# A hybrid decoder layer on one core: a recurrent block's end, the sample states, two recurrences and the last gates are put at other places

## The chip, the core and the metric

The kernel runs on one core of one Trainium2 chip. The core has a matrix engine (TensorE, PE in the profile; its weight loads are listed as PEld), a vector engine (VectorE, DVE), a scalar engine with function tables (ScalarE, ACT), a general one (GpSimd, POOL) and one that only issues transfers (SyncE, SP). Each runs its own instructions in order; semaphores tie them together. Matrix products accumulate in eight banks of PSUM, everything else works from SBUF; the large tensors lie in HBM and come and go by DMA. The metric is the device time of one launch in microseconds (us), less is better.

## What is computed

One layer with two groups of heads over 2048 prompt positions and 8 single-token samples, model width 1024. Cut to what matters here:

```python
hn = _rmsnorm(x, g_norm) * (1.0 + scale[:, None]) + shift[:, None]
z = hn @ w_in
xa, za, q, k, v, glr, zg = jnp.split(z, SPLITS, axis=-1)
# RG-LRU: 8 blocks of 128 channels
xc = conv_b + sum(xp[:, j:j + T] * conv_w[j] for j in range(CONV_W))
gx = jax.nn.sigmoid(xb @ w_gate_x + b_gate_x)          # per block
ga = jax.nn.sigmoid(xb @ w_gate_a + b_gate_a)
a = jnp.exp((LRU_C * ga) * jax.nn.log_sigmoid(lru_lambda))
u = jnp.sqrt(-jnp.expm1(2.0 * log_a)) * (gx * xc)
h = scan(a, u)                                          # h_t = a_t h_{t-1} + u_t
y_lru = h * jax.nn.silu(za)
# GLA: 4 heads, key width 128, value width 256
o, S_new = _gla_chunked(q, k, v, log_alpha, S0)         # S_t = diag(alpha_t) S_{t-1} + k_t^T v_t
o = o * lax.rsqrt(mean(o * o) + EPS) * g_gla_norm
y_gla = o * jax.nn.silu(zg)
x = x + gate * (concat(y_lru, y_gla) @ w_out)
```

The samples take the same layer with their own states: for each of the 8 samples and 4 heads a 128x256 state is read, updated and written.

## The kernel before

The prompt goes in two halves of 1024 positions. Each half walks over the four GLA heads, and puts RG-LRU blocks between them; a segment is 512 positions wide, or 384, 384 and 264 in the second half, where the 8 samples ride along at the end (in some blocks of the first half 512, 256 and 264). A projection (`project`, L661 to L663) is 24 matmuls into one accumulator bank: each operand is split into a high and a low part, and three of the four products are taken. Four PSUM banks rotate as `acc`, two as `tp`, and one each belongs to the head recurrence under the names `kv` and `o`.

An RG-LRU block projects its channels (`xa_unit`), convolves them on DVE (`conv`, L1278), splits the result into `xh` and `xl`, and multiplies these by two gate matrices (`gates`, L1315 to L1317); ACT takes the tanh of both (L1318). When the last segment's gates are in, `gates` goes on to the block's end: an exponential, a tanh and a square root on ACT (L1323, L1325, L1326, the last under another function table), three element-wise steps and the scan on DVE (L1330 to L1334). `out` (L1352) then multiplies the state by the gate value silu(za), which stands in one of four `zs` tiles, and `spill` (L675) sends the product to HBM from ACT's queue.

A head of the GLA group has its decays and its keys and queries (`gla_qk`), then the chunked recurrence: `gla_start` (transposes L1042 and L1045), one `gla_chunk` (L1068 to L1076) for each 128 positions, `gla_norm`, `gla_out` (transposes L1162). In the second half the samples' states follow: `sample_state` loads four states, ACT and DVE update them (L1104, L1105), `sample_out` multiplies them by the queries (L1114), writes them back, and after the second four takes the norm `os` that `gla_out` puts behind the last segment (L1164).

The order of the work on each engine is not that of the source alone. `after(n, f)` puts the function f into a list that falls due n units later, and `tick()`, called after each projection of up to 512 columns, advances the clock and calls what is due. A scheduler then orders each engine's instructions by estimated times; `behind(q)` holds an instruction's place after the last one that engine q has been given so far.

Between the halves some products are made in a cheaper way from sums of blocks of hn (`seven`): seven products instead of eight (named ZB11 to ZT4, matmuls L1559), whose operands are sums and differences of parts of hn that `sums` makes on DVE and ACT (L1491 to L1500, tiles `fs`, `ra`, `so`). The first such group is the gate values of a head (`gates_seven(0)`); the second is the channels of RG-LRU block 0 of the second half (`lru_seven(0)`), whose sums L1568 are written into the block's `xa` tile. `xa_new` makes the tiles of a block and puts the last three columns of the first half at the front of `xa` (L1385). There is one `xa` tile, so a new block writes where the one before it wrote. The last first-half RG-LRU block, number 7, ends shortly before, among the sums.

After the second half's heads, the last two RG-LRU blocks run together (`last_a`): their gates for all three segments are taken at once. `xp`, `lp`, `gp`, `sp_`, `st` are pools of SBUF tiles; the query weights of the first head stand in a tile `wq` of `st`, made at L471.

Of the kernel before, what the change touches and what calls it, by code (L numbers as in the profile page):

```python
# [8 lines left out]
F32 = mybir.dt.float32  # L9
# [5 lines left out]
P = 128  # L15
# [39 lines left out]
def hybrid_kernel(ctx, tc, i, o):  # L55
# [381 lines left out]
    with tc.tile_pool(name="ada", bufs=1, side="right") as ap:  # L437
# [31 lines left out]
        for t in range(2):  # L469
            SP.dma_start(xt45[t], i["x_prompt"][0, (4 + t) * P:(5 + t) * P])  # L470
        wkq0.append(weights(Q0 + HEADS[0] * DK, DK, both=st.tile([P, 2, D], F32R, name="wq"), later=True))  # L471
        x67 = x_pair(2)
# [240 lines left out]

    def flush_gla():
        while any(e[3] for e in pend):
            e = min(e for e in pend if e[3])
            pend.remove(e)
            heapq.heapify(pend)
            e[2]()

    def ada_gate():
# [369 lines left out]
    def sample_state(h, smp, b0, st, done):  # L1091
# [9 lines left out]
        for n in range(4):  # L1101
# [68 lines left out]
    def gla_head(half, h, wv=None, ahead=None):  # L1170
# [57 lines left out]
        for s in range(ns):  # L1228
            if wv and s == 0:
                prep[s] = prep0  # L1230
                pk = project(wk, 512, 512)
                rest()
            else:
                prep[s] = gla_qk(half, h, s, wq, wk, dec, pk)
                pk = None
                if s == 0 and ahead:
                    with held(V):
                        ahead()
            if s + 1 < ns:
# [22 lines left out]
    def lru_units(half, last_a=None, seven=False):  # L1262
# [42 lines left out]
        def gates(t, ss):  # L1305
            j, cv, xh, xl, wgh, wgl, res = t.j, t.cv, t.xh, t.xl, t.wgh, t.wgl, t.res
            if ss[0] == 0:
                t.tx, t.tg = t_("tx"), t_("tg")
            tx, tg = t.tx, t.tg
            for s in ss:  # L1310
                c0, sn = t.segs[s]
                c = slice(c0, c0 + sn)
                for g, (out, bias) in enumerate(((tx, hbx), (tg, hba))):
                    ps = acc()[:, :sn]
                    PE.matmul(ps, wgh[:, g], xh[:, c], start=True, stop=False)  # L1315
                    PE.matmul(ps, wgh[:, g], xl[:, c], start=False, stop=False)
                    PE.matmul(ps, wgl[:, g], xh[:, c], start=False, stop=True)  # L1317
                    S.activation(out[:, c], ps, AF.Tanh, bias=bias[:, j:j + 1], scale=0.5)  # L1318
# [88 lines left out]
        def za_unit(t, s):  # L1407
            c0, sn = t.segs[s]
            z = xp.tile([P, 512], F32, tag="f512", name="z5") if half == 1 and t.j == LRU_TILES[3][0] and s == 2 else None
            z = silu2(t.wz, c0, sn, z)  # L1410
            after(2, lambda: out(t, s, z))
            tick()

        if seven:
            return xa_load, xa_new, xa_unit, out
        return xa_load, xa_unit, za_load, za_unit
# [209 lines left out]
    def lru_seven(j):  # L1626
        xa_load, xa_new, xa_unit, out = lru_units(1, seven=True)
        t = xa_load(j, [None])
# [9 lines left out]

        seven(len(HEADS) - 1 + j, use, lambda s: t.xa[:, 3 + s * 512:3 + s * 512 + 512])

# [618 lines left out]
```

## Time and profile before

| | |
|---|---|
| median of 3 runs | 1452.09 us (1451.66 to 1459.42) |
| the profiled execution, its whole time | 1452.05 us |
| its span in the profile | 1450.3 us, mean granted TensorE clock 0.997 |
| PE matmuls busy | 1425.6 us, 8741 of them |
| DVE, ACT, POOL busy | 1051.2, 690.0, 220.5 us |

Two numbers in a line are the start and the length in us; in square brackets stands how long the engine sat idle before it, and what ended that. In the list of waits a line gives the waiting engine and line, what it waited for, and then the sum in us, the number of times and the longest.

### The profile page before, as it was taken

What the parts mean: (1) busy time and instruction counts of PE and PEld (TensorE: products, weight loads), DVE (VectorE), ACT (ScalarE), POOL (GpSimd) and SP (SyncE); (2) the same over time, 40 slices, a digit from 0 to 9 for tenths busy, and PEclk for the clock granted to TensorE, in tenths of its full rate; (3) what the DMA queues carried; (4) which work ended last, traced back from release to release, by engine and by line L of the source; (5) the groups of instructions that cost most, each with busy time, mean ns of one, the idle gap of its engine ahead of it and who ended that gap; (6) DMA issues with size and microseconds to landing.
All of it is one profiled execution on the core that took longest, in us unless ns stands there. A gap on an engine that the chain in (4) does not pass through costs nothing. (4 is left out here: it accounts for less than half of the span.)

```text
span 1450.3 us, 23579 instructions
## 1 busy us (share of the span) xinstructions
PE 1425.6 (98%) x8741; PEld 1253.1 (86%) x8741; DVE 1051.2 (72%) x2477; ACT 690.0 (48%) x1251; POOL 220.5 (15%) x364
## 2 busy tenths in 40 slices
PE   8999999999999999999999999999999999999998
PEld 6888989899898988878999998999998887788886
DVE  5757658776676688955458687686888986688886
ACT  4644544662545358624354544535557522144342
POOL 0200111212122013100111321433210000000000
PEclk9999999999999999999999999999999999999999
DMA  9755775774665446667844665756672767694453
GB/s 329 267 185 175 259 264 196 251 243 156 200 217 192 160 175 213 204 224 236 293 153 154 201 205 163 244 188 203 213 256 77 279 223 273 229 361 135 135 173 116
DMA packets 161752, 305.33 MB, mean 211 GB/s; under 512 B 12962, under 2 KB 91458, under 8 KB 159197
## 3 DMA queue, kind: packets, MB, share of 16 engines
q1 hardware_dynamic: 106837, 217.39, 44.0%
q0 software_dynamic: 22752, 70.44, 14.3%
q10 hardware_dynamic: 32048, 16.00, 3.7%
q8 instruction: 69, 1.13, 0.3%
q14 instruction: 46, 0.38, 0.1%
HBM read 188.51 MB, written 115.33 MB: 210 GB/s over the span
## 5 line engine op out<-in xcount | busy, mean ns | idle before, releaser
L661 PE MATMUL acc<-hh,w 128*128 128x512 f32 (+3 forms) x1112 | 386.2, 347 | 1.3 <-DVE zs L1129 0.7
L663 PE MATMUL acc<-hh,w 128*128 128x512 f32 (+3 forms) x1112 | 375.6, 338 | 0.0
L662 PE MATMUL acc<-hl,w 128*128 128x512 f32 (+3 forms) x1112 | 375.3, 338 | 0.2 <-DVE hl L205 0.2
L661 PEld LDWEIGHTS acc<-hh,w 128*128 128x128 f32 x1112 | 209.3, 188 | 20.0 <-ACT tx L1318 0.9
L662 PEld LDWEIGHTS acc<-hl,w 128*128 128x128 f32 x1112 | 209.3, 188 | 17.2 <-DVE hl L205 0.5
L663 PEld LDWEIGHTS acc<-hh,w 128*128 128x128 f32 x1112 | 209.1, 188 | 16.8 <-issue 0.4
L1845 PE MATMUL acc<-w,a 128*128 128x512 f32 (+1 forms) x792 | 184.8, 386 | 0.0
L1845 PEld LDWEIGHTS acc<-w,a 128*128 128x128 f32 x792 | 146.8, 188 | 33.2 <-issue 3.4
L346 PE MATMUL acc<-w,hh 128*128 128x256 f32 (+1 forms) x508 | 144.9, 285 | 0.1
L347 PE MATMUL acc<-w,hh 128*128 128x256 f32 (+1 forms) x508 | 143.6, 283 | 0.0
L348 PE MATMUL acc<-w,hl 128*128 128x256 f32 (+1 forms) x508 | 143.6, 283 | 0.0
L1845 PE MATMUL tp<-w,a 128*128 128x512 f32 x564 | 136.0, 391 | 0.0
L1845 PEld LDWEIGHTS tp<-w,a 128*128 128x128 f32 x564 | 105.3, 188 | 26.8 <-issue 5.2
L346 PEld LDWEIGHTS acc<-w,hh 128*128 128x128 f32 x508 | 96.8, 191 | 1.3 <-ACT zs L1128 0.4
L348 PEld LDWEIGHTS acc<-w,hl 128*128 128x128 f32 x508 | 96.4, 190 | 0.0
L347 PEld LDWEIGHTS acc<-w,hh 128*128 128x128 f32 x508 | 95.9, 189 | 0.2
L1128 ACT ACTIVATE zs<-acc 128x512 f32<-128x512 f32 (+3 forms) x70 | 34.5, 492 | 107.4 <-PE acc L663 105.2
L1695 ACT CAST a<-s 128x512 fp32r<-128x512 f32 x61 | 36.5, 619 | 95.9 <-issue 36.6
L1278 DVE SCALAR_TENSOR_TENSOR cv<-xa,vecT,cv 128x512 f32<-128x512 f32 (+2 forms) x120 | 77.1, 645 | 6.0 <-ACT cv L1276 5.7
L1129 DVE SCALAR_TENSOR_TENSOR zs<-zs,acc 128x512 f32<-128x512 f32 (+3 forms) x70 | 38.6, 551 | 47.3 <-ACT zs L1128 47.2
L957 ACT CAST vh<-acc 128x256 fp32r<-128x256 f32 x56 | 20.5, 370 | 83.3 <-PE acc L348 70.0
L958 DVE TENSOR_TENSOR vl<-acc,vh 128x256 fp32r<-128x256 f32 x56 | 23.4, 420 | 43.1 <-ACT vh L957 43.0
(403 smaller groups left out, 2752.0 us busy)
## 6 DMA issues: line engine op xcount, KB each, us to landing
parts<-w SPq DMA_DIRECT2D x37, 1024.0 KB
w<-parts SPq DMA_DIRECT2D x28, 1024.0 KB
wr<-in_w_in_dram SPq DMA_DIRECT2D x38, 512.0 KB
a<-mixd SPq DMA_DIRECT2D x63, 256.0 KB
w<-wd SPq DMA_DIRECT2D x12, 1024.0 KB
w<-twd SPq DMA_DIRECT2D x20, 512.0 KB
mixd<-zs ACTq DMA_DIRECT2D x34, 256.0 KB
wada<-in_w_ada_dram SPq DMA_DIRECT2D x16, 512.0 KB
```

Of the source, the lines that this page charges most:

```text
L346: PE.matmul(ps, hh[:, kt, c], hi[:, kt % 4], start=kt == 0, stop=False)
L347: PE.matmul(ps, hh[:, kt, c], lo[:, kt % 4], start=False, stop=False)
L348: PE.matmul(ps, hl[:, kt, c], hi[:, kt % 4], start=False, stop=kt == KT - 1)
L661: PE.matmul(ps[:, :n], hi[:, kt], a, start=kt == 0, stop=False)
L662: PE.matmul(ps[:, :n], hi[:, kt], b, start=False, stop=False)
L663: PE.matmul(ps[:, :n], lo[:, kt], a, start=False, stop=kt == KT - 1)
L958: V.tensor_tensor(lo, ps[:, :DV], hi.bitcast(F32), op=OP.subtract)
L1128: S.activation(z, ps, AF.Tanh, scale=0.5)
L1129: V.scalar_tensor_tensor(z, z, 1.0, ps, op0=OP.add, op1=OP.mult)
L1278: V.scalar_tensor_tensor(cv[:, cq], xa[:, cq.start + k:cq.stop + k], cw[k], cv[:, cq], op0=OP.mult, op1=OP.add)
L1695: S.copy(t[:, 0, k], (low(t) if src is None else src)[:, k])
L1845: PE.matmul(ps, t[:, u, k], w[:, v, k, c], start=(q < 3 or ps is own) and (k, u, v) == (0, 0, 0), stop=(k, u) == (3, 1), skip_group_check= ...
```

## The change

Six things are changed.

1. The tile `wq` of the query weights is made 56 elements longer and used from element 56 on, so that the weights begin at another address; the tiles of the same pool behind it move by 224 bytes.
2. In the first half the recurrence of the second to fourth head starts two units after its place in the source instead of one, as that of the first head does.
3. The end of block 7 (`chain`, lines taken out of `gates`) is called six units after its gates, and is held behind what DVE and ACT have been given by then. The gate values of this block are put into its own `xa` tile, not into `zs`. Since block 0 of the second half uses the same `xa`, its three front columns (`xa_first`) are now written just before the first of its sums.
4. `flush_gla` sets the clock to each entry's due time while it empties the list.
5. The second four of the samples' states are multiplied four units after their update, not three, and `os` is handed on after one unit, not a half.
6. Of the gates of the last two blocks, the first and the third segment go to the banks `kv` and `o`, as `pg`; the second stays with `acc`.

```diff
@@ -468,7 +468,7 @@
-        wkq0.append(weights(Q0 + HEADS[0] * DK, DK, both=st.tile([P, 2, D], F32R, name="wq"), later=True))
+        wkq0.append(weights(Q0 + HEADS[0] * DK, DK, both=st.tile([P, 2 * D + 56], F32R, name="wq")[:, 56:].rearrange("p (j n) -> p j n", j=2), later=True))
@@ -712,11 +712,14 @@ def flush_gla():
+        now = clock[0]
         while any(e[3] for e in pend):
...
+            clock[0] = max(now, e[0])
             e[2]()
+        clock[0] = now
@@ -1104,7 +1107,7 @@ def sample_state
-        after(3, lambda: sample_out(h, b0, st, s0, done), True)
+        after(4 if b0 else 3, lambda: sample_out(h, b0, st, s0, done), True)
@@ -1217,7 +1220,7 @@ def gla_head
-            sample_state(h, smp, b0, state, lambda: after(0.5, lambda: os_.__setitem__(0, state[1]), True))
+            sample_state(h, smp, b0, state, lambda: after(1, lambda: os_.__setitem__(0, state[1]), True))
...
-                after(2 if h == HEADS[0] else 1, lambda: chunks(0, 0), True, True)
+                after(2 if half == 0 or h == HEADS[0] else 1, lambda: chunks(0, 0), True, True)
@@ -1311,13 +1314,25 @@ def gates
-                    ps = acc()[:, :sn]
+                    ps = (psum.tile([P, 512], F32, tag=("kv", "o")[g], name="pg", bufs=1)
+                          if last_a and s != 1 else acc())[:, :sn]
...
             if ss[-1] < len(t.segs) - 1:
                 return
+            if half == 0 and j == LRU_TILES[3][-1]:
+
+                def late():
+                    with behind(V), behind(S):
+                        chain(t)
+                after(6, late)
+            else:
+                chain(t)
+
+        def chain(t):
+            j, cv, res, tx, tg = t.j, t.cv, t.res, t.tx, t.tg
@@ -1379,6 +1394,10 @@ def xa_new
+            if not seven:
+                xa_first(t)
+
+        def xa_first(t):
             if half == 0:
                 V.memset(t.xa[:, :3], 0.0)
             else:
...
@@ -1407,12 +1426,14 @@ def za_unit
+            if half == 0 and t.j == LRU_TILES[3][-1]:
+                z = t.xa[:, c0:c0 + sn]
             z = silu2(t.wz, c0, sn, z)
@@ -1636,7 +1657,12 @@ def lru_seven
-        seven(len(HEADS) - 1 + j, use, lambda s: t.xa[:, 3 + s * 512:3 + s * 512 + 512])
+        def c2(s):
+            if s == 0:
+                xa_first(t)
+            return t.xa[:, 3 + s * 512:3 + s * 512 + 512]
+
+        seven(len(HEADS) - 1 + j, use, c2)
```

In the changed file lines from about L715 on have numbers 3 to 26 higher; L1345 to L1352 is there what L1330 to L1337 is before, L1367 is L1352, L1404 is L1385, L1516 is L1495, L1580 is L1559, L1589 is L1568.

The order of instructions shows three places. First DVE among the sums, before: the end of block 7 (`tg`, `tx`, the scan with 1024 columns into `tg`, `hc`, and the two products `zs<-tg,zs`) lies between the sums `ra`, `fs` and `so`.

```order
L1331 SCALAR_TENSOR_TENSOR tg<-xl,tg 128x1024 [waits Activation_49]
L1129 SCALAR_TENSOR_TENSOR zs<-zs,acc 128x512 [waits DMAHW7_49,Activation_49]
L1332 TENSOR_TENSOR tx<-tx,tg 128x1024 [waits DVE_49]
L1491 TENSOR_TENSOR ra<-fs_5824,ra 128x1024
L1334 SCALAR_TENSOR_TENSOR tg<-xl,tx 128x1024 [waits DVE_49]
L1129 SCALAR_TENSOR_TENSOR zs<-zs,acc 128x512 [waits DMAHW1_49,Activation_49]
L1337 COPY hc<-tg 128x1 [waits DVE_49]
L1352 SCALAR_TENSOR_TENSOR zs<-tg,zs 128x512 x2
L1491 TENSOR_TENSOR fs_5824<-fs_5823,fs_5824 128x1024
L1495 TENSOR_TENSOR so<-fs_5823,so 128x1024
```

After, the same end stands behind the last of the sums and the gate values, directly ahead of the sums of block 0. The transfers that send `xa` out are counted by two semaphores, and the copy into `xa` waits for them.

```order
L1345 SCALAR_TENSOR_TENSOR tx<-tx,cv 128x1024
L1346 SCALAR_TENSOR_TENSOR tg<-xl,tg 128x1024 [waits Activation_49]
L1347 TENSOR_TENSOR tx<-tx,tg 128x1024 [waits DVE_49]
L1349 SCALAR_TENSOR_TENSOR tg<-xl,tx 128x1024 [waits DVE_49]
L1352 COPY hc<-tg 128x1 [waits DVE_49]
L1367 SCALAR_TENSOR_TENSOR xa<-tg,xa 128x512 x2
L1404 COPY xa<-xac 128x3 [waits DMAHW6_49,DMAHW5_49,DVE_49]
L1589 TENSOR_TENSOR xa<-acc,es 128x512 [waits PE_49,Activation_49]
```

So the end has moved from ahead of the operands of the first group to ahead of `xa<-acc,es`, with a new wait of the copy on the two transfers. On PE, the product into which that sum's bank goes on (first row with a wait on DVE and transfer 0) comes later than before by 21 matmuls, which the scheduler took from products that stood behind it; before, it follows the products with `ra` directly:

```order
L1559 MATMUL acc<-ra,w 128x512
L1559 MATMUL acc<-so,w 128x512 x2
L1559 MATMUL acc<-ra,w 128x512
L1559 MATMUL acc<-so,w 128x512
L1559 MATMUL acc<-hh,w 128x512 [waits DMAHW2_49,DVE_49]
L1559 MATMUL acc<-hl,w 128x512
```

and after, the rows before it are products of `hh` and `hl` into other banks:

```order
L1580 MATMUL acc<-hh,w 128x512 x2
L1580 MATMUL acc<-hl,w 128x512
L1580 MATMUL acc<-hh,w 128x512 x2
L1580 MATMUL acc<-hl,w 128x512
L1580 MATMUL acc<-hh,w 128x512
L1580 MATMUL acc<-hh,w 128x512 [waits DMAHW0_49,DVE_49]
L1580 MATMUL acc<-hl,w 128x512
L1580 MATMUL acc<-hh,w 128x512 x2
```

Second, PE at the end of the first head of the second half: the products of the second four states (`po<-xt,qm`) before stand between the last 264-column projection and the 264-column gates,

```order
L662 MATMUL acc<-hl,w 128x264
L663 MATMUL acc<-hh,w 128x264
L1114 MATMUL po<-xt,qm 32x256 [waits DMASW1_49,DVE_49]
L1114 MATMUL po<-xt,qm 32x256 x3
L1315 MATMUL acc<-xh,wg 128x264
L1316 MATMUL acc<-xl,wg 128x264
L1317 MATMUL acc<-xh,wg 128x264
L1315 MATMUL acc<-xh,wg 128x264 [waits Activation_49]
```

and after they have gone 54 matmuls further, among the projections of the next head's values.

```order
L346 MATMUL acc<-w,hh 128x256
L347 MATMUL acc<-w,hh 128x256
L348 MATMUL acc<-w,hl 128x256
L1117 MATMUL po<-xt,qm 32x256 [waits DMASW1_49,DVE_49]
L1117 MATMUL po<-xt,qm 32x256 x3
L346 MATMUL acc<-w,hh 128x256 [waits Activation_49]
L347 MATMUL acc<-w,hh 128x256
L348 MATMUL acc<-w,hl 128x256
```

Third, PE at the gates of the first of the last two blocks. Before, all six pairs go through `acc`,

```order
L1315 MATMUL acc<-xh,wg 128x384
L1316 MATMUL acc<-xl,wg 128x384
L1317 MATMUL acc<-xh,wg 128x384
L1315 MATMUL acc<-xh,wg 128x384
L1316 MATMUL acc<-xl,wg 128x384
L1317 MATMUL acc<-xh,wg 128x384
L1315 MATMUL acc<-xh,wg 128x264
```

and after, a pair into `kv` and `o` comes on either side of the pair in `acc`.

```order
L1319 MATMUL pg<-xh,wg 128x384
L1320 MATMUL pg<-xl,wg 128x384
L1321 MATMUL pg<-xh,wg 128x384
L1319 MATMUL acc<-xh,wg 128x384
L1320 MATMUL acc<-xl,wg 128x384
L1321 MATMUL acc<-xh,wg 128x384
L1319 MATMUL acc<-xh,wg 128x384
L1320 MATMUL acc<-xl,wg 128x384
L1321 MATMUL acc<-xh,wg 128x384
L1319 MATMUL pg<-xh,wg 128x264
L1320 MATMUL pg<-xl,wg 128x264
```

More of the change, by code (lines that the diff above doesn't have):

```diff
@@ L1305, in gates @@
         def gates(t, ss):
-            j, cv, xh, xl, wgh, wgl, res = t.j, t.cv, t.xh, t.xl, t.wgh, t.wgl, t.res
+            j, xh, xl, wgh, wgl = t.j, t.xh, t.xl, t.wgh, t.wgl
             if ss[0] == 0:
@@ L1414, in lru_units @@
         if seven:
-            return xa_load, xa_new, xa_unit, out
+            return xa_load, xa_new, xa_first, xa_unit, out
         return xa_load, xa_unit, za_load, za_unit
@@ L1626, in lru_seven @@
     def lru_seven(j):
-        xa_load, xa_new, xa_unit, out = lru_units(1, seven=True)
+        xa_load, xa_new, xa_first, xa_unit, out = lru_units(1, seven=True)
         t = xa_load(j, [None])
```

## The prediction

> **What bounds the kernel.** I read the page first.
>
> ```profile
> span 1450.3 us, 23579 instructions
> PE 1425.6 (98%) x8741; PEld 1253.1 (86%) x8741; DVE 1051.2 (72%) x2477; ACT 690.0 (48%) x1251; POOL 220.5 (15%) x364
> ```
>
> PE is busy for 98% of the span, and the change takes no matmul away. What it can give is therefore what PE waits, 1450.3 - 1425.6 = 24.7 us, some of which lies at both ends of the program, and what follows from a wait. The second view is the list of PE's waits; these lines lie where the change does something:
>
> ```profile
> PE po L1114 <- DVE xt L1105: 2.1, 1, 2.1
> PE acc L1559 <- DVE so L1495: 1.4, 2, 1.2
> PE acc L1315 <- DVE zs L1129: 1.4, 1, 1.4
> PE acc L1315 <- ACT tx L1318: 1.1, 1, 1.1
> PE tp L1042 <- DVE xb L1027: 1.0, 1, 1.0
> PE acc L1559 <- DVE ra L1495: 0.8, 1, 0.8
> PE tp L1162 <- DVE on L1089: 0.7, 1, 0.7
> PE acc L661 <- DVE zs L1129: 0.7, 1, 0.7
> ```
>
> They sum to 9.2 us. Half a percent of the kernel, about what a measurement of it can tell from no change, is 7.3 us; so a change that removed all of this and added nothing would be just seen. I then looked at each place by windows and timeline. The one that differs from the rest is the first wait, near 885:
>
> ```profile
> 885.00:887.30 2.30, 0.22 (x2) 0.01 (x1) 1.68 (x4) 1.71 (x4) 0.00 (x0) 1.00 0.31 37
> 887.30:889.00 1.70, 1.66 (x12) 1.02 (x13) 0.69 (x2) 0.00 (x0) 0.77 (x1) 0.59 0.93 373
> 889.00:891.20 2.20, 2.20 (x12) 2.20 (x12) 1.42 (x3) 1.94 (x5) 0.00 (x0) 0.54 1.02 393
> ```
>
> Columns are the window, its length, the busy time of the engines, and then the granted clock (1.00, 0.59, 0.54). After a wait of 2.1 us PE ran at little more than half clock for 3.9 us, which cost 1.70 x 0.41 + 2.20 x 0.46 = 1.7 us more. The waits of 1.0 to 1.4 us have no such stretch behind them.
>
> **The change part by part.** All sums are against the profiled execution, 1452.05 us with its span of 1450.3 us; the median of the runs is 0.04 us higher, which I leave out.
>
> *Query weights.* Only the address changes.
>
> ```profile
> L661 PE MATMUL acc<-hh,wq x16: 392/396/481, 52.9 to 87.3; 128*128 128x512 f32 x16
> L1559 PE MATMUL acc<-so,w x64: 388/389/507, 610.4 to 635.2; 128*128 128x512 f32 x64
> ```
>
> A matmul of 512 columns on `wq` has a median of 396 ns, one of the same shape elsewhere 389. With 48 of them the gain is at most 48 x 7 ns = 0.3 us, and nothing if the stage and not the address makes it. I take 0.2.
>
> *First recurrences.* The start of a head's recurrence, its chunks and its transposes move one projection later in three heads. Only the second head has waits there, 1.0 us before L1042 and 0.7 before L1162; the lists show each just once. A wait also empties PE's pipeline: in the fence on the gates below, the step from 1090.84 to 1092.24 is 1.40 us, against a wait of 1.07 and a normal step of 0.17, so about 0.2 to 0.3 us are lost beside a wait. Both waits are shorter than a projection, and they go: -2.3 us. In the other two heads nothing was waited for, so there is nothing to gain; the moved DVE and ACT work meets the next stage instead, and I cost that at nothing, because DVE has 28% of its time free there as elsewhere. If that cover fails, each of the moved steps can become a wait of the size just named (first rival). Bounds -2.3 and +5.
>
> *Samples.* The chain of work that ended last passes through this wait:
>
> ```profile
> 879.94 4.99 DMA xt<-in_state_gla_dram
> 885.01 0.52 ACT xt L1104
> 885.56 1.70 DVE xt L1105 x4
> ```
>
> The states land at 884.9 and are ready at 887.3, while PE was ready at 885.1. After, 54 matmuls stand between, six gates and 48 of the next head's values, some 6 us of work; that is more than the 2.2 us needed. What moves with the matmuls is the write-back of the states on POOL's queue, one unit later, where it holds the tile of the states that long, and the norm of `os` on DVE, which now lies in the stage of the values. The wait of 2.1 goes, and with it the half clock (1.7) and 0.2 for the pipeline: -4.0 us; between -2.1, if the clock falls anyway, and -4.2.
>
> *Gates of the last two blocks.* PE, then ACT, in the timeline:
>
> ```profile
> 1089.97 0.33 PE L1315 MATMUL acc<-xh,wg 128*128 128x384 f32 x1
> 1090.84 0.34 PE L1317 MATMUL acc<-xh,wg 128*128 128x384 f32 x1
> 1092.24 0.44 PE L1315 MATMUL acc<-xh,wg 128*128 128x384 f32 x1 [1.07 <-ACT tx L1318]
> 1094.92 0.39 PE L661 MATMUL acc<-hh,w 128*128 128x264 f32 x1
> ```
> ```profile
> 1091.62 0.58 ACT L1318 ACTIVATE tx<-acc,hbx 128x384 f32<-128x384 f32 x1
> 1092.09 0.57 ACT L1318 ACTIVATE tg<-acc,hba 128x384 f32<-128x384 f32 x1
> 1110.77 0.57 ACT L1318 ACTIVATE tx<-acc,hbx 128x384 f32<-128x384 f32 x1
> ```
>
> Eighteen gate matmuls took 1094.92 - 1089.97 = 4.95 us. Five steps from 1089.97 to 1090.84 make 0.174 us each, so 12 of them at 0.174 and six narrower at 264/384 of it take 2.8: 2.1 us are lost. After, the four wide pairs run through to 1092.06; the third segment needs `kv` and `o`, free once ACT has read them at 1092.20 and 1092.66. ACT stays where it was, so about 0.2 us of wait, the restart, and something like 0.2 for the next projection's bank remain: 1.5 us go. In the second block PE waits 1.4 us for DVE to empty an `acc` bank. The two new banks cover the first segment, but the second segment still takes two `acc` banks, 0.5 us later than the first did, so I let 0.2 to 0.3 of the wait stand: 1.2 go. Together -2.7; bounds -0.5 (ACT, which starts its tanh at 1110.77, is the limit after all) and -3.5.
>
> *The end of block 7.* Three waits of L1559 (so 1.4 in two, ra 0.8) go, since DVE no longer has these rows among the sums:
>
> ```profile
> 601.02 1.22 DVE L1331 SCALAR_TENSOR_TENSOR tg<-xl,tg 128x1024 f32<-128x1024 f32 x1
> 605.02 2.29 DVE L1334 TENSOR_TENSOR_SCAN tg<-xl,tx 128x1024 f32<-128x1024 f32 x1
> 607.86 1.29 DVE L1352 SCALAR_TENSOR_TENSOR zs<-tg,zs 128x512 f32<-128x512 f32 x2
> ```
>
> With the three steps of the kind of the first row that is over 7 us that leaves DVE ahead of the sums; 2.2 us of waits and 0.2 for each restart make -2.8. The wait of 0.7 for `zs` L1129 before the sums stays or grows, because more of the normalisation's DVE steps now stand ahead of it: +0.5 (0 to 1.1).
>
> What is late next is the end itself. On ACT:
>
> ```profile
> 591.71 1.25 ACT L1323 ACTIVATE xl<-tg,lc 128x1024 f32<-128x1024 f32 x1
> 595.22 1.23 ACT L1325 ACTIVATE tg<-tg,lc 128x1024 f32<-128x1024 f32 x1
> 596.47 1.28 ACT L1326 ACT_TABLE_LOAD   x1
> 597.76 1.06 ACT L1326 ACTIVATE tg<-tg 128x1024 f32<-128x1024 f32 x1
> 627.98 0.64 ACT L1128 ACTIVATE zs<-zs 128x512 f32<-128x512 f32 x1
> ```
>
> The chain now starts after the last of these, the tanh of a gate value. In before's clock, less 2.8 us, that ends at 625.8, and up to 0.9 earlier, since a bank copy (0.57) that stood ahead of it now stands behind; take 625.1. Exponential, copy, tanh, table and root add 1.25 + 0.57 + 1.23 + 1.28 + 1.06 = 5.4, so the root is there at 630.5. On DVE 1.22 + 1.22 + 2.29 + 1.29 follow: 636.5, and ACT issues the two transfers of `xa` at about 636.0 and 636.6. Then the copy into `xa` waits until both have landed. DVE works in order, so `xa<-acc,es` and all behind it wait too, and PE's product that goes on in that bank waits for this sum. How long such a transfer takes:
>
> ```profile
> 522.38 0.37 ACTq L675 DMA_DIRECT2D mixd<-zs  x1
> q10 hardware_dynamic: 1056, 0.52, 75.7%
> 608.58 1.10 ACTq L675 DMA_DIRECT2D mixd<-zs  x2
> q10 hardware_dynamic: 528, 0.26, 23.6%
> zgd<-zs POOLq DMA_DIRECT2D x4, 256.0 KB, 4.3
> ```
>
> The second row is ACT's queue from 522 to 524.3: two transfers, the second issued at 522.38, were through within 1.9 us, with no other queue moving. The fourth is the same queue from 614.5 to 618.2: half of the pair issued at 608.6 to 609.2 moved only then, so that one took up to 9.0 us, behind the loads of SP. The last is POOL's queue from 600 to 650, same size, with 4.3 us from issue to landing; I take that, being of this stage and this size. So 636.6 + 4.3 = 640.9, plus copy and sum (0.15 and 0.69 by like rows) 641.8. When is PE there?
>
> ```profile
> 631.81 1.30 PE L1559 MATMUL acc<-so,w 128*128 128x512 f32 x5
> 635.44 0.39 PE L1559 MATMUL acc<-hh,w 128*128 128x512 f32 x1
> ```
>
> In before the product starts at 635.44. Less 2.8, plus the 21 matmuls that the order puts ahead of it, at 0.227 us (four steps of the first row make 1.30 - 0.39), PE is ready at 637.4. It waits 4.4 us, more than the 2.1 that cost the clock at 885, so another 1.7. The next sum into `xa` has only four matmuls to hide behind, +0.3. The part comes to -2.8 + 0.5 + 4.4 + 1.7 + 0.3 = +4.1 us. With landing in 1.9 us, and the chain a little earlier, the wait is 1.5 and the clock stays: -0.5. With 9.0 us it is 9.1: +8.8.
>
> [...]
>
> *`flush_gla`'s clock* moves the last heads' steps only where entries come due out of order; no row of PE has moved there by it that I found: 0.
>
> Sum: -0.2 - 2.3 - 4.0 - 2.7 + 4.1 = -5.1, so 1452.05 - 5.1 = 1447.0 us.
>
> **The rivals.**
>
> *The later recurrences collide* (slower). Place: the second to fourth head of the first half, where the transposes L1042 and L1162 now come one projection later, next to the convolution of a block. Against it, none of these places waits before except in one head. For it, the waits there were DVE's (xb, on), and DVE's work only moves. Price: about 1.2 us with the restart for each wait; five of them (6 us) take the change beyond before's time, and with six it is 1447.0 + 7.2 = 1454.2. Chance 0.12, half of it beyond 1459.3.
>
> *The transfers land early, or the chain does.* Then the wait for `xa` is 1.5 us, PE keeps its clock, and the sum is -0.2 - 2.3 - 4.0 - 2.7 - 0.5 = -9.7: 1442.4. For it: the pair at 522. Against: SP's queue is loading operands at 632 to 640 as it was at 609. Chance 0.28.
>
> *They land as late as at 609.* +8.8 in place of +4.1: 1451.7. Chance 0.08.
>
> *Gates and samples do not do what they say.* ACT is the limit of the gates (-0.5), and the clock at 885 falls for another reason (-2.1): 1447.0 + 2.2 + 1.9 = 1451.1. Chance 0.10. [...]
>
> **How the numbers follow.** The forecast's own case has 0.42, from 1445 to 1449 us by the bounds of the transfer's landing between 2.6 and 6 us. Faster by over 0.5% (below 1444.8) takes the early landing, 0.28, and 0.06 from the forecast's lower end: 0.34. Slower by over 0.5% (above 1459.3) is half the collision, 0.06. The rest, 0.60, is within 0.5%. From 1441.5 to 1453 the range takes in the early and the late landing, and leaves out most of the collision and gains beyond those summed here.
>
> **What would show it.** Each step has its line: no wait of L1114's successor on `xt` and no stretch below full clock at 880; no waits on `xb` and `on` near 188 and 225; under 0.5 us each at the gates; none on `so` and `ra`, and one of some 4 us on `xa` near 640 with a stretch of half clock behind it. I am wrong if that one is under 1 us, if waits on `xb` or `on` come up in other heads, or if `zs` before the sums grows beyond 1.8 us.

## The result, and the profile after

The changed kernel runs at 1457.36 us (median of 22 runs, 1453.93 to 1462.57) against 1453.16 us for the kernel before (22 runs beside them). The ratio is 1.0028, with a 95% interval of 1.0019 to 1.0036. It is slower, by 0.3%; 1447.0 us had been forecast, with 1441.5 to 1453.0 us as the range. The profiled execution took 1457.12 us, 5.07 more than that of the kernel before. Its page begins:

```profile
span 1455.3 us, 23575 instructions
PE 1429.1 (98%) x8741; PEld 1256.6 (86%) x8741; DVE 1052.6 (72%) x2477; ACT 689.9 (47%) x1251; POOL 220.8 (15%) x364
```

The matmuls are the same 8741, and PE's busy time has grown by 3.5 us nevertheless, since stretches at half clock count as busy, and there are three of 3.41 us here against one before. The waits of PE in the changed kernel (us in all, times, longest):

```profile
PE tp L1167 <- DVE os L1127: 5.7, 4, 2.3
PE acc L1580 <- DVE xa L1589: 3.0, 1, 3.0
PE acc L1320 <- DVE xl L1299: 1.9, 1, 1.9
PE acc L661 <- DVE f L1005: 0.8, 1, 0.8
PE pkv L1073 <- DVE kTl L1055: 0.6, 1, 0.6
```

The waits on `xt`, `so`, `ra` of L1559, `zs`, `tx`, `xb` and `on`, which the prediction quoted from before, are all gone. Four others have come, and the one on `os`, which before was a single one of 0.8 us in the last head, is now the largest; the sum did not have it. Behind the longest wait on `os` and those on `xa` and `xl` PE runs at half clock for 3.41 us each, which the windows of 4 us cut across (window, its length, busy times, then granted clock, DMA share, GB/s):

```profile
640.00:644.00 4.00, 3.39 (x11) 2.72 (x12) 3.35 (x5) 0.82 (x1) 0.00 (x0) 0.77 0.00 0
644.00:648.00 4.00, 4.00 (x16) 3.18 (x15) 2.13 (x5) 1.81 (x3) 0.00 (x0) 0.81 0.42 135
908.00:912.00 4.00, 4.00 (x23) 4.00 (x22) 3.51 (x12) 0.37 (x1) 2.22 (x5) 0.57 0.68 217
1116.00:1120.00 4.00, 3.81 (x13) 3.51 (x14) 3.39 (x10) 0.88 (x2) 1.22 (x2) 0.57 0.33 131
```

To see where the time went, I took the start of the same matmuls in each trace: the product from which a head's decays are made (`acc<-gls,g2s`), the first of heads 2 and 4 of the first half, the first and the last one of the second half, and the first product of the statistics of the last stage (`pss<-raw,mixs`). They cut the span into six stages; the last is 248.2 to 248.3 us long in every trace and is left out. Lengths in us, from the traces, and in the last column the median of all runs:

| kernel | start to head 2 (weights) | to head 4 (recurrences) | to second half (block 7's end) | second half's heads (samples) | last gates | median of runs |
|---|---|---|---|---|---|---|
| before | 175.5 | 263.6 | 298.1 | 286.0 | 178.8 | 1453.2 |
| after | 175.6 | 263.2 | 300.6 | 289.5 | 178.2 | 1457.4 |
| samples undone | 175.4 | 263.4 | 300.7 | 283.8 | 178.2 | 1454.5 |
| product in the state | 175.5 | 263.6 | 298.2 | 290.6 | 177.0 | 1456.2 |
| `os` after 2 units | 175.5 | 263.3 | 299.3 | 281.3 | 178.0 | 1451.5 |
| gates undone | 176.6 | 263.2 | 301.7 | 288.6 | 179.7 | 1459.8 |
| `os` after 2, end undone | 176.7 | 263.5 | 298.6 | 283.9 | 177.0 | 1449.5 |
| the same, banks in one block | 176.1 | 263.1 | 298.7 | 283.1 | 177.3 | 1448.4 |
| `os` after 2, first end held | 175.7 | 263.1 | 300.6 | 281.8 | 176.3 | 1448.0 |
| `os` after 2, end and recurrences undone | 176.7 | 264.2 | 298.3 | 285.3 | 177.6 | 1451.6 |
| before, recurrences alone | 176.7 | 263.3 | 298.6 | 285.9 | 178.4 | 1452.7 |
| `os` after 2, end undone, first end held | 176.3 | 263.6 | 298.4 | 283.0 | 176.5 | 1448.8 |
| block 7's end after 5 units | 177.0 | 263.2 | 297.3 | 281.2 | 176.8 | 1445.5 |
| block 7's end after 4 units | 176.0 | 263.2 | 299.4 | 284.6 | 176.1 | 1449.2 |

From before to after the stages moved by +0.1, -0.4, +2.5, +3.5 and -0.6 us. The first column varies by 1.7 us over programs that hardly differ in that stage, so a stage says more than a single execution's total. Its cause is not shown: PE's waits there on loads of `wada` differ too, but do not follow it (1.7 us of them where the column has 175.5, 1.0 where it has 176.7).

The stages are those of one execution each, and that of `os` after 2 units is the shortest of its eleven (1447.47 us). The rows from the third on were run in three groups of four, beside which the kernel before had medians of 1453.13, 1453.58 and 1453.95 us; across groups it is the ratios to it that compare.

### The profile page after: what moved, and what is told of

Read it like the earlier page. It is cut to its first block, busy times and chain, and to the rows that moved or that the text cites. A ratio compares the mean times of both kernels' runs of the same rounds, so it can differ in the third digit from the quotient of the medians.

```text
span 1455.3 us, 23575 instructions
## 1 busy us (share of the span) xinstructions
PE 1429.1 (98%) x8741; PEld 1256.6 (86%) x8741; DVE 1052.6 (72%) x2477; ACT 689.9 (47%) x1251; POOL 220.8 (15%) x364
```

## What the trace shows in the three stages

*The samples.* The wait on `xt` is gone as forecast. But in each of the second half's first three heads PE now comes to the transposes of `os` (L1167) before DVE has normalised it. DVE's timeline in the second head (start, duration, engine and line, operation; in brackets the idle time before it and what ended it):

```profile
899.85 0.41 DVE L1122 TENSOR_TENSOR os<-os,po 128x256 f32<-128x256 f32 x1
900.18 2.34 DVE L1349 TENSOR_TENSOR_SCAN tg<-xl,hc,tx 128x1024 f32<-128x1024 f32 x1
902.50 0.14 DVE L147 TENSOR_SCALAR rs_x<-oss 128x1 f32<-128x1 f32 x1
906.15 0.16 DVE L153 SCALAR_TENSOR_TENSOR ors<-rs_t,rs_y 128x1 f32<-128x1 f32 x1
906.34 0.35 DVE L1127 TENSOR_SCALAR os<-os,ors 128x256 f32<-128x256 f32 x1
```

and PE's:

```profile
904.19 0.28 PE L348 MATMUL acc<-w,hl 128*128 128x256 f32 x1
906.75 0.61 PE L1167 MATMUL tp<-sel,os 128*128 128x8 f32 x4 [2.29 <-DVE os L1127]
907.22 0.36 PE L346 MATMUL acc<-w,hh 128*128 128x256 f32 x1
```

The last sum of `os` ends at 900.26. Then DVE does the scan of the second-half block (2.34 us), that block's two products, and twelve small steps of the inverse root, which stand between other work; `os` is there at 906.69. In the kernel before, PE came to the same transposes at 895.98 without a wait, ahead of that block's scan at 899.05:

```profile
895.98 0.29 PE L1164 MATMUL tp<-sel,os 128*128 128x8 f32 x2
899.05 2.34 DVE L1334 TENSOR_TENSOR_SCAN tg<-xl,hc,tx 128x1024 f32<-128x1024 f32 x1
```

Handing `os` on one half unit later was less than the delay of its norm. The three new waits, in the first three heads, are 1.46, 2.29 and 1.07 us; the fourth, 0.88 us in the last head, had stood before with 0.83.

*Block 7's end.* The chain came almost as forecast, here on DVE and then PE:

```profile
630.28 1.23 DVE L1346 SCALAR_TENSOR_TENSOR tg<-xl,tg 128x1024 f32<-128x1024 f32 x1 [3.34 <-ACT tg L1341]
635.19 1.28 DVE L1367 SCALAR_TENSOR_TENSOR xa<-tg,xa 128x512 f32<-128x512 f32 x2
639.76 0.17 DVE L1404 COPY xa<-xac 128x3 f32<-128x3 f32 x1 [3.29 <-DMA mixd<-xa]
639.86 0.69 DVE L1589 TENSOR_TENSOR xa<-acc,es 128x512 f32<-128x512 f32 x1
640.61 0.50 PE L1580 MATMUL acc<-hh,w 128*128 128x512 f32 x1 [2.96 <-DVE xa L1589]
```

DVE stands for 3.29 us after the products until the transfers to HBM have landed, and PE waits 2.96 us for the sum behind them.

*The last gates.* Because the first of the two last blocks now has its gates earlier, its scan moved ahead of the second block's convolution on DVE. Before, it stood behind the convolution's steps, of which the last `cv<-xa` was at 1104.02:

```profile
1104.02 0.48 DVE L1278 SCALAR_TENSOR_TENSOR cv<-xa,vecT,cv 128x256 f32<-128x256 f32 x1
1107.31 2.35 DVE L1334 TENSOR_TENSOR_SCAN tg<-xt,hc,tx 128x1024 f32<-128x1024 f32 x1
```

and after:

```profile
1111.06 0.55 DVE L1299 TENSOR_TENSOR xl<-cv,xh 128x384 fp32r<-128x384 f32 x1
1111.53 2.35 DVE L1349 TENSOR_TENSOR_SCAN tg<-xt,hc,tx 128x1024 f32<-128x1024 f32 x1
1115.05 0.48 DVE L1281 SCALAR_TENSOR_TENSOR cv<-xa,vecT,cv 128x256 f32<-128x256 f32 x1
1115.58 0.55 DVE L1299 TENSOR_TENSOR xl<-cv,xh 128x384 fp32r<-128x384 f32 x1
1116.18 0.44 PE L1320 MATMUL acc<-xl,wg 128*128 128x384 f32 x1 [1.90 <-DVE xl L1299]
```

The gates of the second block's next segment need the `xl` of 1115.58, which stands behind the scan, and PE waits 1.90 us in the middle of that group.

## The experiments

**The samples.** First the two edits to the samples were taken out of the changed kernel:

```diff
-        after(4 if b0 else 3, lambda: sample_out(h, b0, st, s0, done), True)
+        after(3, lambda: sample_out(h, b0, st, s0, done), True)
...
-            sample_state(h, smp, b0, state, lambda: after(1, lambda: os_.__setitem__(0, state[1]), True))
+            sample_state(h, smp, b0, state, lambda: after(0.5, lambda: os_.__setitem__(0, state[1]), True))
```

> The changed kernel with the second four sample states multiplied three units after their update again, and their norm handed on after half a unit, as before the change. Theory: the new waits of PE on os (5.7 us in four places, and a stretch at half clock behind the longest) come from the changed distance between these products and the matmul that needs os. Then they go, the wait of 2.1 us on xt and its half clock come back, and the heads of the second half take what they took before: 3.5 us less than in the changed kernel, about 1453.9 us. Rival: DVE is late there because of the other parts of the change; then the waits on os stay and the time is within 1 us of the changed kernel's 1457.4.

Measured 1454.5 us, ratio to before 1.0009 (1.0000 to 1.0019). The stage fell from 289.5 to 283.8 us, and of the waits on `os` one of 0.6 us was left, while one of 1.5 us stood before the products of `xt` again. Unlike the wait at this place before the change, it had no half clock behind it, and this trace is 2.2 us shorter there than that of the kernel before. So the samples' edits made the changed kernel slower, by 2.9 us in the medians.

Then only the hand-over of `os` was put later still, with the products of the samples left late:

```diff
-            sample_state(h, smp, b0, state, lambda: after(1, lambda: os_.__setitem__(0, state[1]), True))
+            sample_state(h, smp, b0, state, lambda: after(2, lambda: os_.__setitem__(0, state[1]), True))
```

> The changed kernel with os handed on after two units, not one: PE's matmuls on os move about 35 matmuls further back, DVE's order stays. Theory: os is ready about 2 us after PE asks for it, so with 4 us more in between the waits in the first three heads of the second half go (4.8 of 5.7 us), and the half clock behind one of them (1.7 us): 6 us less than the changed kernel, about 1451.3 us. Rival: the later end of a head's last segment holds tiles that the next head needs, and waits come up there; then the gain is 2 us or less.

Measured 1451.49 us, ratio 0.9986 (0.9976 to 0.9996). DVE's order differs only in the steps that follow from the moved transposes. The list of PE's waits:

```profile
PE acc L1580 <- DVE xa L1589: 2.9, 1, 2.9
PE acc L1320 <- DVE xl L1299: 1.9, 1, 1.9
PE tp L1167 <- DVE os L1127: 0.7, 1, 0.7
```

The waits on `os` fell from 5.7 to 0.7 us and the stage to 281.3 us, which is 4.7 less than in the kernel before, where -4.0 had been forecast; the wait that is left is that of the last head. By the medians the step took off 5.9 us; the stages of the two traces differ by 8.2. In the seven other traces with `os` after 2 units the stage is 281.2 to 285.3 us, so the gain against before is 0.7 to 4.8 us: 281.2 and 281.8 where block 7's end is 5 or 6 units late, 283.0 to 285.3 where it is earlier, with waits of 0.9 to 2.1 us on `w`, `f`, `mid` or `S` that the others don't have. Why the end's place should matter there is not shown. That the samples' part had a gain, and that a place in PE's order one unit too early turned it into a loss, is.

**Block 7's end.** If the wait for the transfers is what costs, the last product can be written over the recurrence's state, and nothing waits for HBM:

```diff
-            V.scalar_tensor_tensor(z, h[0][:, c0:c0 + sn], 0.5, z, op0=OP.mult, op1=OP.mult)
-            spill(z, j, half, c0, sn)
+            y = h[0][:, c0:c0 + sn] if half == 0 and j == LRU_TILES[3][-1] else z
+            V.scalar_tensor_tensor(y, h[0][:, c0:c0 + sn], 0.5, z, op0=OP.mult, op1=OP.mult)
+            spill(y, j, half, c0, sn)
```

> The changed kernel, but the last product of block 7 is written over the state in tg and goes to HBM from there; xa is then read by DVE alone, and the copy into xa waits for no transfer. Theory: the 3.0 us that PE waits near 637 are the landing of the two transfers. Then DVE makes the sum 3.2 us earlier, PE waits under 0.3 us, there is no stretch at half clock behind it, and the kernel is 3.0 + 1.7 = 4.7 us faster than the changed one: about 1452.7 us. Rival: the block's end is itself too late for PE, whatever its transfers do; then a wait of 1 us or more stays and the gain is 2 us or less.

Measured 1456.2 us, ratio 1.0021 (1.0011 to 1.0031): 1.2 us less than the changed kernel, where 4.7 were expected, and the two intervals overlap; the rival (a gain of 2 us or less) was right. The sum does start 3.3 us earlier, but the scheduler, which reckons with that, puts 12 matmuls fewer ahead of it, and PE is there earlier too:

```profile
636.52 0.69 DVE L1590 TENSOR_TENSOR xa<-acc,es 128x512 f32<-128x512 f32 x1
637.27 0.50 PE L1581 MATMUL acc<-hh,w 128*128 128x512 f32 x1 [2.33 <-DVE xa L1590]
```

The landing was on the path, but taking it off leaves a wait of 2.33 us for the chain itself. In this trace no half clock followed that wait; the stage is as long as before the change (298.2 us). Next, with `os` after 2 units in all that follow, block 7's end went back to where it was:

```diff
-            if half == 0 and j == LRU_TILES[3][-1]:
-
-                def late():
-                    with behind(V), behind(S):
-                        chain(t)
-                after(6, late)
-            else:
-                chain(t)
+            chain(t)
```

> The changed kernel with the samples' outputs handed on after 2 units (the run before this, 1451.5 us) and, beside that, block 7's end where it was. Theory: the late end cost 2.5 us between 577 and 748 us of the changed kernel's trace (a wait of 3.0 us on xa and the half clock behind it, less the waits on so and ra that it removed), so this runs at 1449.0 us. Rival: what the late end costs at its own place comes back behind it, because the DVE has its 6 us of work out of the way of the sums, and the time stays at 1451.5 us (1450.8 or more speaks for the rival).

Measured 1449.54 us, ratio 0.9973 (0.9963 to 0.9982), so the late end costs 2.0 us in the medians, though the two intervals overlap, and 0.7 in the profiled stage, where no half clock followed the wait on `xa` in the run that it is compared with. The traced execution as a whole is 2.3 us longer than that one, since the second half's heads and the start took longer.

**The gates.** The idle banks were taken out of the changed kernel:

```diff
-                    ps = (psum.tile([P, 512], F32, tag=("kv", "o")[g], name="pg", bufs=1)
-                          if last_a and s != 1 else acc())[:, :sn]
+                    ps = (psum.tile([P, 512], F32, tag=("kv", "o")[g], name="pg", bufs=1)
+                          if False else acc())[:, :sn]
```

> The changed kernel with all gates of the last two blocks in the four rotating banks again. Theory: the idle banks let the first of the two blocks end earlier in the order, which puts its scan ahead of the second block's convolution on DVE, and PE then waits 1.9 us for xl and runs at half clock behind it; against that stand the waits for banks that went. The stage gave 0.6 us in one profile, so without the idle banks the kernel is 0.6 us slower than the changed one, about 1458, and DVE's scan stands behind the convolution's last steps again. Rival: the wait on xl is DVE's load and comes back with the old banks too; then the kernel is 2 us or more slower than the changed one.

Measured 1459.8 us, ratio 1.0046 (1.0033 to 1.0059). The wait on `xl` is not in its list, and the old two are back:

```profile
PE acc L1319 <- DVE zs L1132: 1.4, 1, 1.4
PE acc L1319 <- ACT tx L1322: 0.9, 1, 0.9
```

The time is one that the rival named (2 us or more above the changed kernel), but the wait on `xl` by which it was to come is not there. So the idle banks are a gain, 1.5 us in the stage and 2.4 in the medians (the intervals just overlap), and the wait on `xl` is their doing. Two runs took that wait away in different ways. In the first only the second block's gates use the idle banks (`if last_a and s != 1 and j == LRU_TILES[3][2]`), and block 7's end is where it was:

> As the run with block 7's end where it was, but only the second of the two last blocks has its gates in the idle banks; the first has them in acc's again. Theory: the DVE order puts the first block's scan (2.35 us) behind the second block's last convolution steps again, so the wait of 1.9 us on xl and the half clock behind it go, and the second block's group still loses nothing to acc's ring: 1447.5 us, 1.5 us under the run with both blocks in the idle banks. Rival: the first block's group then loses what it lost before the change (1.4 us on zs and 0.9 on tx), and the time stands at 1449.0 to 1450.0 us.

Measured 1448.4 us, ratio 0.9968 (0.9957 to 0.9979), between the two expectations and not clear of the run with both blocks (0.9973): the wait of 1.9 us on `xl` is gone, 0.2 us being left, a wait of 0.9 us on `tx` is back, and the stage is no shorter than with both blocks (177.3 against 177.0). In the second both blocks keep the idle banks, block 7's end is late, and the first block's end is held:

```diff
+            elif last_a and j == LRU_TILES[3][1]:
+
+                def held_end():
+                    with behind(V):
+                        chain(t)
+                after(2, held_end)
             else:
                 chain(t)
```

> The changed kernel with the samples' outputs handed on after 2 units, block 7's end late as the change has it, both blocks' gates in the idle banks, and the end of the first of the two last blocks held back by 2 units so that its scan stands behind the second block's xl on the DVE. Theory: the wait on xl (1.9 us and 0.6 of half clock) goes and nothing takes its place, since the products of that block are not needed for several units: 1449.0 us, against 1451.5 with the end not held. Rival: the held end is late for something else (its products' units, or the second block's end behind it), and a wait of 2 us or more on it stands in the last 250 us: 1451.5 us or more.

Measured 1447.96 us, ratio 0.9975 (0.9961 to 0.9989). DVE in its trace:

```profile
1105.24 0.42 DVE L1299 TENSOR_TENSOR xl<-cv,xh 128x264 fp32r<-128x264 f32 x1
1107.19 2.34 DVE L1355 TENSOR_TENSOR_SCAN tg<-xt,hc,tx 128x1024 f32<-128x1024 f32 x1
```

The scan stands behind the last `xl`, the wait of 1.9 us is gone (one of 1.1 on `tx`, before the second block's group, has come), and the stage is 176.3 us: 1.7 less than with the end not held, of which the half clock is a part, and 2.5 less than before the change. The gain of 2.7 us that the prediction gave to the gates is nearly there once the scan no longer stands ahead of the `xl`.

**The recurrences.** They were put back in the run with `os` after 2 units and block 7's end undone (first edit), and made alone on the kernel before (second):

```diff
-                after(2 if half == 0 or h == HEADS[0] else 1, lambda: chunks(0, 0), True, True)
+                after(2 if h == HEADS[0] else 1, lambda: chunks(0, 0), True, True)
...
-                after(2 if h == HEADS[0] else 1, lambda: chunks(0, 0), True, True)
+                after(2 if half == 0 or h == HEADS[0] else 1, lambda: chunks(0, 0), True, True)
```

> As the run with block 7's end where it was, and the first half's recurrences of heads 2 to 4 after 1 unit as before. Theory from the traces: the later recurrences moved the PE by 0.4 us in all (waits of 1.34 and 1.06 us go, one of 0.73 us on kTl comes), so this runs at 1449.4 us against 1449.0. Rival, the term as it was predicted: they are worth 2.3 us, and this runs at 1451.3 us.

> The kernel before with the first half's recurrences of heads 2 to 4 after 2 units, and nothing else. Theory from the traces: two waits of 1.34 and 1.06 us go at the head of a stage, one of 0.7 us on kTl comes, and what is saved later is given back where the PE runs into other waits of the same heads: the PE is 0.4 to 0.7 us ahead at 577 us, and the time is 1453.0 us (0.9997 of the kernel before). Rival, the term as predicted: 2.3 us, 1451.2 us, a ratio of 0.9984 or less.

The first took 1451.61 us, ratio 0.9990 (0.9979 to 1.0001), which is 2.1 us more than the run that it undoes and so speaks for the term as predicted, though the intervals of the two overlap. The second took 1452.65 us, ratio 0.9998 (0.9989 to 1.0007), and speaks against it. The stages decide where to look: in the first 0.7 of its profile's 2.3 us lie in the recurrences' own stage, and 1.4 lie in the second half's heads, where DVE's and PE's orders are the same in both programs; there a wait of 2.1 us on `S` stands where the other run waits 0.9 us on `f`. In the second the own stage is 0.3 us shorter than before. So the edit is worth 0.3 to 0.7 us in its place. Why two programs with the same order there wait for different steps I don't know; that stays open.

**The parts together.** Then the two gains were put in one kernel, block 7's end undone and the first of the last blocks held:

> The samples' outputs handed on after 2 units, block 7's end where it was before the change, and the first of the last two blocks' end held by 2 units. If the costs are separate, both gains add: block 7's end gave 2.0 us (1451.5 to 1449.5), the held end 3.5 us (1451.5 to 1448.0), together 1446.0 us. Rival: they are not separate (the early start of the later stages is lost again at a wait on a transfer of w, which stood at 827 us in the run with block 7's end back): 1448.0 us or more.

Measured 1448.82 us, ratio 0.9965 (0.9953 to 0.9977). That is 2.8 us more than expected, but the expectation put medians of different groups together. By the ratios the two steps are 0.9986 to 0.9973 and 0.9986 to 0.9975, which together give 0.9962, and 0.9965 does not speak against it. In their own stages the gains are both there: 298.4 us at block 7's end and 176.5 us at the last gates, against 298.6 and 176.3 in the runs with one of them. Other stages are longer than in the run with the first end held: 1.2 us in the second half's heads, where a wait of 1.1 us on `mid` has come, and 1.2 us in the start and the recurrences' stage. The wait on `w` that the rival named is not in this trace.

Last, block 7's end was kept late but less late, with the product in the state and the first end held; only the number in `after(6, late)` differs between the two runs:

> As the run with the first end held (1448.0 us; block 7's end after 6 units, a wait of 2.9 us on xa), but block 7's end after 5 units and its products written where no transfer to HBM is waited for. Theory: what the late end costs is its place in the DVE's order alone, and one unit earlier is enough: the wait on xa is under 1 us, those on so and ra stay away, and the time is 1446.0 us. Rival: the sums move back with it, and the wait of 2 us or more comes up under another name (so, ra or zs): 1448.0 us.

> As the run after 5 units, but after 4. Theory: at 4 units part of the end stands among the sums, and the sums of the last tiles wait for it: a wait of 1 to 2.5 us on so or ra comes back, 1447.5 us. Rival: the DVE has slack there, no wait over 1 us is left between 600 and 650 us, and the time is 1445.5 us.

After 5 units: 1445.51 us, ratio 0.9947 (0.9934 to 0.9961), the lowest median of all (its interval still meets those of the runs around it). After 4 units: 1449.23 us, ratio 0.9967 (0.9955 to 0.9979). DVE and PE after 5 units:

```profile
616.13 1.22 DVE L1351 SCALAR_TENSOR_TENSOR tx<-tx,cv 128x1024 f32<-128x1024 f32 x1
621.78 2.28 DVE L1355 TENSOR_TENSOR_SCAN tg<-xl,tx 128x1024 f32<-128x1024 f32 x1
624.62 1.29 DVE L1374 SCALAR_TENSOR_TENSOR tg<-tg,xa 128x512 f32<-128x512 f32 x2
633.23 0.69 DVE L1596 TENSOR_TENSOR xa<-acc,es 128x512 f32<-128x512 f32 x1 [3.21 <-PE acc L1587]
621.92 0.50 PE L1587 MATMUL acc<-hh,w 128*128 128x512 f32 x1 [1.27 <-DVE zs L1596]
```

The end now starts right behind the last of the sums of hn's parts (`ra<-fs,so` at 613 in this trace) and is over at 625.9; at 633.23 it is DVE that waits for PE, not PE for DVE. One wait of 1.27 us is left, on `zs`, and no half clock follows; the stage is 297.3 us, 0.8 less than before the change and 3.3 less than after. After 4 units the end mixes with the sums:

```profile
610.45 0.50 PE L1587 MATMUL acc<-hh,w 128*128 128x512 f32 x1 [2.03 <-ACT acc L1601]
```

The wait is of the size expected (1 to 2.5 us), though the trace names ACT's copy and not `so` or `ra`: on ACT the table load and the root of the end (607.56 to 609.91) stand ahead of this copy. The clock fell behind it (0.62 from 612 to 616). Of the 3.7 us between the two medians the stage of block 7's end has 2.1; the second half's heads, where PE's order is the same in both, are 3.4 us longer after 4 units, and the start is 1.0 shorter. After 6 units, with the same product in the state but the rest of the changed kernel, that stage had 298.2 us.

## Why the prediction was wrong, step by step

- *Samples: the step that failed*, forecast -4.0 and measured +3.5 us. The removed wait was right, the cost of what moved was not. The prediction said that "the norm of `os` on DVE" now "lies in the stage of the values" and gave it no price; it asked whether 6 us of matmuls cover the states, and not how long after them PE asks for `os`. Three new waits on `os` of 4.8 us in all and one of 0.8 us on `f`, with a half clock behind the longest, took the place of the wait of 2.1 us on `xt` with its half clock: 4.8 + 0.8 - 2.1 = 3.5. Without them, with `os` after 2 units, one trace shows -4.7, and the others -0.7 to -4.8. Of the -4.0, 1.7 was the half clock of a single trace; with the recurrences alone, where the samples are as before, a wait of 1.9 us at this place had none behind it.
- *Gates*: forecast -2.7, measured -0.6. The banks did what was said (their own loss is gone), but the prediction reckoned with ACT and the banks alone. It did not see that DVE's scan changes places with the convolution, which brought a new wait of 1.9 us and a half clock. With the scan held the stage gives -2.5.
- *Recurrences*: forecast -2.3, measured -0.4 in their stages. Both waits went, which with the restart had cost 1.34 and 1.06 us; new is one of 0.6 us on `kTl` at 201 us, in the second head, and the rest is given back in small pieces. The rival of collisions in the other heads did not come: `xb` has no wait left, and `on` only one of 0.3 us, in the second half. The prediction took 0.2 to 0.3 us for the restart beside a wait from a row that gives 1.40 - 1.07 - 0.17 = 0.16; at these two waits it was 0.38 and 0.35. (A second small misreading: before the wait on `xt` PE was ready at 885.2, not 885.1.)
- *Block 7's end*: forecast +4.1, measured +2.5: the mechanism held, the sizes were off. The wait on `xa` is 2.96 us instead of 4.4, since the landing took 3.3 us from the end of the products and not 4.3 from the later issue. No run shows the landing of 2.6 us that the forecast's own case has as its lower bound; the traces have more, from the end of the products on: in the run without idle banks DVE waited 4.3 us for the same transfers and in the one with the first end held 3.2, so no single figure holds. The wait on `zs` before the sums went instead of growing by 0.5, and small waits of 0.7 us on `ra` in hn's transposes came, which the sum did not have. The half clock behind the wait came as forecast, in part by luck: with `os` after 2 units a wait of the same size on `xa` (2.93 us) had none.
- *Query weights*: forecast -0.2. Their matmuls went from a median of 396 ns to 391:

```profile
L661 PE MATMUL acc<-hh,wq x16: 388/391/477, 53.0 to 87.3; 128*128 128x512 f32 x16
```

That is 48 x 5 ns = 0.24 us, as forecast, and too little to be seen in the stage. It goes with the address: the median of this row is 389 to 391 ns in all twelve traces with the new one, and 396 and 395 in the two with the old (before, and the recurrences alone). For `flush_gla`'s clock nothing speaks for a cost other than the forecast 0; it was not tried alone.

The differences add up to the miss: 7.5 (samples) + 2.1 (gates) + 1.9 (recurrences) - 1.6 (block 7's end) + 0.3 (start) = 10.2 us, against 5.07 + 5.1 = 10.2. The range failed for the same reason as the sum: the only rival that went beyond the time before was the later recurrences, and no case had a delayed operand of the samples in it. None of the three signs of being wrong that the prediction named came up either: the wait on `xa` is not under 1 us, the other heads have none on `xb` or `on`, and the one on `zs` did not grow.

## What to carry to other kernels

When a step is moved later, follow each of its results to the instruction that needs it: a wait that is taken from the operand's side can come back on the result's side, here in three heads instead of one. Where a scheduler orders the engines, an earlier start of one chain can put its long step (here a scan of 2.3 us) ahead of a short step that another engine waits for, so look at the whole order of the engine that serves PE, not at the moved rows. Moving a serial chain can have a best place between two worse ones, so try the neighbours of the place chosen: 1445.5 us after 5 units, 1449.2 after 4, and 1448.0 after 6 (there with the transfers waited for, so not a run that differs in the place alone).

## What was unexpected of the hardware

The half clock behind a wait of PE came in about half of the cases. Over all 14 traces, from 40 us on and up to the last stage, 41 waits of 0.9 to 1.45 us have no slow stretch behind them. Of 25 waits from 1.46 to 3.94 us, 13 have one; by the clock's record in the traces each lasts 3.41 us, at half clock, which is 1.7 us of matmul time. The same wait of 1.9 us on `xl` has one in three traces and none in three others, and 2.93 us on `xa` had none in the run with `os` after 2 units where 2.96 us had one in the changed kernel.

So in these traces the length of a wait alone does not settle whether a stretch follows. Of the eleven waits over 2 us eight have one behind them. In the run with the product in the state the 2.33 us on `xa` have none, while two of the waits on `os`, 1.6 us at the longest, have one each. What else it hangs on is left open.

The 1.7 us that the prediction put behind each wait of over 2 us is the right price where a stretch comes, and it came behind eight of the eleven. Such stretches can be part of why runs of one kernel lie several us apart (1453.93 to 1462.57 for the changed one): over its 22 runs a mean granted clock lower by 0.001 went with 1.1 us more (correlation -0.65), where such stretches alone would make 1.5 (1.7 us for each 0.0012). In the fastest kernel no wait after the start reaches 1.45 us.
